# Attention transfers in program order, gate outputs from ScalarE's queue, a dilated merge over more slots, and a first head laid elsewhere

## The chip, the cores and the metric

The kernel runs on one core of one Trainium2 chip. The metric is the device time of one execution in microseconds (us); lower is better. All data are float32; the matmuls take their operands as two parts each (a rounded high part and the rest), so one product is three matmuls: high by high, high by low, low by high.

The engines are named as in the profile: PE is TensorE (PEld its weight loads), DVE is VectorE, ACT is ScalarE, POOL is GpSimd, SP is SyncE, which here only issues transfers. ACT can issue transfers too.

## The reference, cut to what matters

One layer of a bidirectional encoder on a sequence of 1024 positions with a width of 1024:

```python
h = rmsnorm(x, g_mix) * (1 + scale1) + shift1
qa, ka, va, qb, kb, vb, ga, gb = split(h @ w_in)         # 6 x 512 columns, then 2 x 1024 gate columns
oa = mixture_of_dilations(qa, ka, va, rel_bias)          # 8 heads of 64, windows (128,1), (512,4), (2048,16)
ob = neighbourhood_attention_2d(qb, kb, vb, rpb)         # 8 heads of 64, an 8 x 16 window on a 16 x 64 grid
merged = sigmoid(ga) * (oa @ w_branch_dil) + sigmoid(gb) * (ob @ w_branch_na)
x = x + gate1 * (merged @ w_out)
# then rmsnorm, an up projection, a depthwise convolution, a gated product, a down projection, rmsnorm
```

The three dilated patterns of a head are merged for each position by softmax weights over their log sums (`w = softmax(lse)`, `sum(w * o)`).

## The kernel before

The program is traced from Python into one instruction list per engine. A planner places the instructions: it simulates the program and lets an engine's later instruction go ahead of an earlier one where that looks better. Inside `tc.manual_schedule(engines=...)` the engines named keep the order in which the program was written. Waits are put in by the planner. Every transfer counts on one of eight completion counters, given out in turn over both issuing engines, and it waits for the transfer that had the same counter before, so a transfer waits for the landing of the one eight places ahead of it in the planned order.

The stages that matter here, with their times in the profile:

1. *Projections* (to 281 us). Seven pairs of q and k products (`order = (4, 5, 6, 7, 1, 2, 3)`) are computed with a seven-product scheme; `a_operands` prepares the weights of one pair mostly on POOL (sums at lines 441 to 443, subtractions at line 61). Their raw weights come by `p_load` (line 708) alternately into the buffers `wraw` of the pool `w` and `xr` of the pool `lpool`, two buffers each. Results are staged in `qs` tiles and stored from ACT's queue to the scratch tensor `qks` (lines 375 and 393). At the end the first two gate weight tiles (`w_in[24]`, `w_in[25]`) are loaded into `wraw` (line 833).
2. *First loads of the attention* (lines 843 to 853). The pools of the projection are released, and new pools take their place from the same address on: `qk2` (q, k and low k of two heads, each tile 4 KB a partition), then `sm` (the multiplier `lnm`, four `bias` tiles, two `vv` tiles, the probabilities `P`), and, later in the text, `at` (operands `th` and `tl`, outputs `u1` and `u23`, the merge's small tiles `fr`, `fs`, `fa`, `fl`, `fb`). A tile waits for whatever lay at its place before. The first head's loads are written in the order `qk_load(0)`, `lnm`, bias, values, second bias.
3. *Attention* (281 to about 650 us). 102 slots are run in order, each as `settle` (softmax of the scores of the slot before on DVE and ACT, copies of turned tiles), then the lists `first`, `O`, `T`, `S`, `last` of that slot. Eight dilated heads, in four pairs, start eight slots apart (slots 0 to 63 and a tail); eight neighbourhood heads start at slots 64, 68 and so on, four apart. Between the parts of a slot `fill` puts steps of the gate product (`h @ w_in` columns 24 to 39, 256 steps of three matmuls), so that PE has work. After a gate tile of 128 x 512 is done, ACT copies it to a `gs` tile (two buffers, line 1309) and SP stores it to the scratch tensor `gs` (line 1310). ACT, DVE and PE keep program order here; SP and POOL are planned freely.
4. *Merge of a dilated pair*, whose first slot is `s0 = 16 * pr`: `turn` (transpose of the statistics, s0 + 17), `rows` (copy to `fr`, store to the scratch `sts`, line 1121), `spread` (nine reads back in another layout, lines 1125 and 1129, s0 + 19), `factors` (s0 + 20, DVE line 1135 first), `shares` (s0 + 21, ten stores of the weights to `fcs`), `load` (broadcast reads into `fb`), `weigh` (DVE line 1167) and `merge` (POOL line 1176 and the store of the output, line 1177, s0 + 31).
5. *Branch stage* (from about 650 us): outputs are read back (`oraw`), split, and multiplied by `w_br`; gates are read back and passed through a sigmoid.

In the merge the slots are fixed numbers; DVE waits inside `factors` for the reads of `spread`.

Of the kernel before, what the change touches and what calls it, by code (L numbers as in the profile page):

```python
# [10 lines left out]
FT = mybir.dt.float32  # L11
# [8 lines left out]
KT = 8  # L20
# [9 lines left out]
def hybrid_encoder(tc, xT, c, w_ada, small, w_in, p1_bias, p23_bias, na_bias, ln2_mult, ident, w_br, w_out,  # L30
# [57 lines left out]
    halves = [slice(0, 512), slice(512, 1024)]  # L88
# [435 lines left out]
    with tc.manual_schedule(engines={e.engine for e in (sp, act, dve, pool, pe)}):  # L524
# [183 lines left out]
        def p_load(n):  # L708
            pr, r = order[n], []
            for t in (pr, 4 + pr) if pr < 4 else (8 + pr, 12 + pr):  # L710
                r.append(wpool.tile([128, KT, 128], FT, name="wraw") if n % 2 == 0 else
                         lpool.tile([128, KT, 128], FT, name="xr", bufs=2))
                sp.dma_start(r[-1], w_in[t])
            return [t.rearrange("p (a b) m -> p a b m", a=2) for t in r]
# [126 lines left out]
    lpool.release()  # L841
    qkpool.release()
    qk2 = tc.alloc_tile_pool(name="qk2", bufs=2, reuse_waits="tile")
    sm_pool = tc.alloc_tile_pool(name="sm", bufs=2, reuse_waits="tile")
    with tc.manual_schedule(engines={sp.engine, pool.engine}):
        qks = {0: qk_load(0)}
# [28 lines left out]
        act.activation(pp, pp, AF.Exp, bias=mi, scale=-1.0, accum_out=li)  # L875

    gspool = tc.alloc_tile_pool(name="gs", bufs=2, side="right", reuse_waits="tile")
    at_pool = tc.alloc_tile_pool(name="at", bufs=2, reuse_waits="tile")

    turned, scored = [], []  # L880

# [74 lines left out]
    def at(slot, phase, job, *args):  # L956
        slots[slot][phase].append((job, args))

    class DilHead:
        def __init__(self, pair, pr, i, s0, u, st):  # L960
            self.pair = pair
            self.pr, self.i, self.u, self.st, self.head = pr, i, u, st, 2 * pr + i
            self.a = slice(64 * i, 64 * i + 64)
            self.P, self.tt, self.po = {}, {}, {}
            if self.head > 1:
                at(s0 - 5, "first", self.load)
                at(s0 - 8, "first", lambda: qks.update({self.head: qk_load(self.head)}))
            if self.head:
                at(s0 - 3, "first", self.load_v)
                at(s0 - 2, "first", self.prepare)  # L970
                at(s0 - 1, "first", lambda: q_blocks(qks[self.head]))
            at(s0, "first", self.values)
            for n in range(4):
                at(s0 + n, "S", self.far_scores, n)
                at(s0 + n + 2, "T", self.far_turn, n)
                at(s0 + n + 4, "O", self.far_out, n)
                at(s0 + n + 4, "S", self.near_scores, n)
                for js in (((0, 1),), ((2, 3),), ((4, 5),), ((6, 7), (8,)))[n]:
                    at(s0 + n + 6 + (js == (8,)), "T", self.near_turn, js)
                    at(s0 + n + 8 + (js == (8,)), "O", self.near_out, js)  # L980
# [112 lines left out]
    class DilPair:  # L1093
        def __init__(self, pr):
            self.pr, s0 = pr, 16 * pr
            at(s0, "first", self.begin) if pr else self.begin()
            for i in range(2):
                DilHead(self, pr, i, s0 + 8 * i, lambda: self.u, lambda: self.st)
            at(s0 + 17, "T", self.turn)
            at(s0 + 20, "last", self.factors)  # L1100
            at(s0 + 19, "first", self.spread)
            at(s0 + 21, "last", self.shares)
            for z in range(2):
                at(s0 + 22 + z, "first", self.load, 1, z)
            for n, g, z in ((25, 1, 0), (26, 1, 1), (29, 0, 0), (30, 0, 1)):
                at(s0 + n, "last", self.weigh, g, z)
            at(s0 + 31, "first", self.merge)

        def begin(self):
            self.u = [at_pool.tile([128, S], FT, name=n) for n in ("u1", "u23")]  # L1110
# [179 lines left out]
    def fill_steps():  # L1290
# [3 lines left out]
        for n in range(16):  # L1294
# [6 lines left out]
            for hf in range(2):  # L1301
                ensure(marks[-2])
                p = ps_g.tile([128, 512], FT, name="pj")
                for k in range(KT):
                    product(p, w, lambda k: h[hf, k], ks=[k])
                    if k == KT - 1:
                        def out(p=p, n=n, hf=hf):
                            g = gspool.tile([128, 512], FT, name="gs")
                            act.activation(g, p, AF.Copy)
                            sp.dma_start(g_scr[n][:, halves[hf]], g)  # L1310
                        aside(600, out)
                        marks.append(count[0])
                    yield
# [11 lines left out]
    def fill(n, asides=True):  # L1325
        for _ in range(n):
            next(steps, None)
            if asides:
                catch_up(550)
# [4 lines left out]

    att = contextlib.ExitStack()
    att.enter_context(tc.manual_schedule(engines={e.engine for e in (pe, act, dve)}))
    fill(5)
    for s in range(102):
        n = 2 + (s % 4 == 3) if s < 64 else 2 + s % 2 if s < 96 else 1
# [6 lines left out]
        run(slots[s]["last"])  # L1346
        fill(n - (n > 1))
    ensure(count[0])
    at_pool.release()
    sm_pool.release()  # L1350
    ps_a.release()
    ps_l.release()
    qk2.release()
# [62 lines left out]
    mpool = tc.alloc_tile_pool(name="mg", bufs=1, side="right", reuse_waits="tile")  # L1416
    ms = [mpool.tile([128, KT, S], FR, name=n) for n in ("mhi", "mlo")]

    sp_order = contextlib.ExitStack()
    sp_order.enter_context(tc.manual_schedule(engines={e.engine for e in (sp, pool)}))  # L1420
    late = [(j, t) for j in (10, 11) for t in range(KT)]
# [651 lines left out]
```

## Time and profile before

| | |
|---|---|
| median of 3 runs | 1502.94 us (1498.84 to 1503.26) |
| profiled execution, its own time | 1502.36 us |
| its span, first to last instruction | 1500.6 us |
| TensorE busy | 1451.0 us, 97% of the span |
| ScalarE, VectorE, GpSimd busy | 53%, 64%, 56% |
| mean granted TensorE clock | 0.989 |
| transfers | 241.14 MB, mean 161 GB/s |
| share of transfers issued by SP (q1) and ACT (q10) | 220.04 and 19.73 MB |

A row of the timeline has the start in us, the duration in us, the engine, the line of the kernel, the operation, and output <- input with the number of instructions merged; in brackets stands how long the engine had been idle before, and whom it waited for. `SPq` and `ACTq` are the queues that issue transfers; an issue is not the transfer's own time. A row of waits has the waiting group, the group waited for, the sum in us, the number of times and the longest. A row of stretches has the stretch, its length, the busy time of PE, PEld, DVE, ACT and POOL with their instruction counts, the granted TensorE clock (1.00 is full speed), the mean busy share of the 16 DMA engines, and GB/s.

### The profile page before, as it was taken

Reading aid. Unit: us, or ns where it says so; the run is one execution under the profiler, and the core shown is the slowest. Engines: PE = TensorE matmul, PEld = TensorE weight load, DVE = VectorE, ACT = ScalarE, POOL = GpSimd, SP = SyncE. Lnnn points to the kernel's source line nnn. Section 1 sums busy time; section 2 is a strip of 40 time slices with the busy share of each in tenths; the row PEclk is TensorE's granted clock in tenths of the full one; section 3 lists DMA queues with packets and bytes.
Section 4 is the critical chain, followed back from the end, with each engine's and each line's share of the span. In section 5 each row is a group of like instructions: output and inputs, shape, how many; then the busy total and the mean of one; then the engine's idle time right before and its main releaser. Section 6 shows DMA issues by size and latency. Waiting matters only on the chain.

```text
span 1500.6 us, 21335 instructions
## 1 busy us (share of the span) xinstructions
PE 1451.0 (97%) x7308; PEld 1225.1 (82%) x7308; DVE 967.5 (64%) x1809; ACT 790.4 (53%) x1479; POOL 839.4 (56%) x690
## 2 busy tenths in 40 slices
PE   9999999799999699999999999999999999999998
PEld 8877888688888578887888778888888888887788
DVE  7696543256666476657625798666666667787865
ACT  6635543277777466763335555444444447574542
POOL 4165675244451365522257858766666676988712
PEclk9999999899999899999999999999999999999999
DMA  9596345676777989668744413222222234542313
GB/s 368 204 345 210 101 180 197 201 188 164 185 194 190 235 199 265 177 222 271 232 133 154 133 43 107 93 84 77 85 76 85 85 133 143 197 142 69 99 46 113
DMA packets 130516, 241.14 MB, mean 161 GB/s; under 512 B 47812, under 2 KB 60740, under 8 KB 130372
## 3 DMA queue, kind: packets, MB, share of 16 engines
q1 hardware_dynamic: 121752, 220.04, 47.9%
q10 hardware_dynamic: 8656, 19.73, 3.5%
q8 instruction: 58, 0.95, 0.3%
q14 instruction: 50, 0.41, 0.1%
HBM read 185.60 MB, written 59.90 MB: 164 GB/s over the span
## 4 chain that ended last, share of the span: by engine, by line
PE 67%; DMA 9%; DVE 8%; POOL 6%; ACT 5%; issue 3%; SPq 1%; ACTq 0%; DVEq 0%; POOLq 0%
PE pj L497 13%; PE pj L495 13%; PE pj L496 13%; PE pj L84 6%; PE pj L86 6%; PE pj L85 6%; PE T L1021 1%; PE O L1033 1%; POOL wlo L61 1%; DMA oraw<-ob 1%; POOL wsl L61 1%; DMA wraw<-w_down 1%; DMA oraw<-w_ada 1%; PE T L1069 1%; DMA ks<-qks 1%
## 5 line engine op out<-in xcount | busy, mean ns | idle before, releaser
L61 POOL TENSOR_TENSOR wlo<-wraw,whi 128x512 fp32r<-128x512 f32 (+1 forms) x92 | 116.8, 1290 | 132.3 <-ACT whi L57 114.9
L495 PE MATMUL pj<-op,wsh 128*128 128x512 f32 x408 | 158.5, 390 | 1.8 <-ACT wsh L57 1.8
L496 PE MATMUL pj<-op,wsh 128*128 128x512 f32 x408 | 158.9, 390 | 0.5 <-DVE op L1492 0.5
L497 PE MATMUL pj<-op,wsl 128*128 128x512 f32 x408 | 157.4, 389 | 0.0
L61 POOL TENSOR_TENSOR wsl<-big,wsh 128x512 fp32r<-128x512 f32 (+1 forms) x86 | 111.7, 1320 | 45.0 <-ACT wsh L57 40.0
L84 PE MATMUL pj<-h,whi 128*128 128x512 f32 x272 | 117.7, 433 | 0.0
L85 PE MATMUL pj<-h,whi 128*128 128x512 f32 x272 | 108.4, 399 | 0.0
L86 PE MATMUL pj<-h,wlo 128*128 128x512 f32 x272 | 108.2, 398 | 0.0
L1702 DVE SCALAR_TENSOR_TENSOR big<-pj,sm,big 128x512 f32<-128x512 f32 (+2 forms) x183 | 94.9, 563 | 16.5 <-ACT big L1696 15.5
L889 DVE TENSOR_TENSOR tl<-T,th 128x512 fp32r<-128x512 f32 (+3 forms) x120 | 76.1, 649 | 25.9 <-ACT th L885 25.9
L495 PEld LDWEIGHTS pj<-op,wsh 128*128 128x128 f32 x408 | 76.6, 188 | 18.5 <-ACT wsh L57 2.7
L495 PE MATMUL pj<-op,whi 128*128 128x512 f32 x232 | 90.7, 391 | 0.3 <-ACT wc L501 0.3
L496 PE MATMUL pj<-op,whi 128*128 128x512 f32 x232 | 90.5, 390 | 0.2 <-DVE op L1522 0.2
L496 PEld LDWEIGHTS pj<-op,wsh 128*128 128x128 f32 x408 | 76.6, 188 | 17.0 <-DVE op L1492 0.9
L497 PE MATMUL pj<-op,wlo 128*128 128x512 f32 x232 | 90.3, 389 | 0.0
L497 PEld LDWEIGHTS pj<-op,wsl 128*128 128x128 f32 x408 | 76.6, 188 | 15.9 <-POOL wsl L61 0.2
L61 POOL TENSOR_TENSOR wsl<-wraw,wsh 128x384 fp32r<-128x384 f32 (+1 forms) x46 | 56.7, 1254 | 57.7 <-ACT wsh L57 50.0
L874 DVE CUSTOM_DVE_ANT_0 P<-S,bias 128x256 f32<-128x256 f32 x128 | 48.9, 420 | 56.0 <-PE S L1006 36.1
L57 ACT ACTIVATE whi<-wraw 128x1024 fp32r<-128x1024 f32 (+2 forms) x49 | 48.5, 994 | 57.7 <-PE pj L85 28.9
L1250 POOL TENSOR_SCALAR P<-P,stb 128x288 f32<-128x288 f32 (+1 forms) x32 | 41.2, 1286 | 65.4 <-DVE stb L1247 28.1
L875 ACT ACTIVATE P<-P,st 128x256 f32<-128x256 f32 x128 | 64.0, 503 | 25.8 <-DVE st L874 25.6
L1696 ACT ACTIVATE big<-pj,sm 128x512 f32<-128x512 f32 x61 | 47.0, 773 | 54.5 <-DVE pj L516 32.2
(476 smaller groups left out, 4546.6 us busy)
## 6 DMA issues: line engine op xcount, KB each, us to landing
wada<-w_ada SPq DMA_DIRECT2D x31, 512.0 KB
qks<-qs ACTq DMA_DIRECT2D x28, 512.0 KB
wraw<-w_in SPq DMA_DIRECT2D x26, 512.0 KB
big<-w_up SPq DMA_DIRECT2D x22, 512.0 KB
wraw<-w_up SPq DMA_DIRECT2D x22, 512.0 KB
big<-as SPq DMA_DIRECT2D x22, 512.0 KB
as<-big SPq DMA_DIRECT2D x21, 512.0 KB
qs<-qks SPq DMA_DIRECT2D x32, 256.0 KB
```

The costliest lines, as they stand in the source:

```text
L57: act.activation(hi, raw, AF.Copy)
L61: lo_eng.tensor_tensor(lo[:, i:i + step], raw[:, i:i + step], f(hi)[:, i:i + step], OP.subtract)
L84: pe.matmul(psum, whi[:, k0 + k], mhi, start=k == 0, stop=False)
L85: pe.matmul(psum, whi[:, k0 + k], mlo, start=False, stop=False)
L86: pe.matmul(psum, wlo[:, k0 + k], mhi, start=False, stop=k == n - 1)
L495: pe.matmul(psum, whi[:, k], bhi, start=j < 4 and k == 0, stop=False, skip_group_check=True)
L496: pe.matmul(psum, whi[:, k], blo, start=False, stop=False, skip_group_check=True)
L497: pe.matmul(psum, wlo[:, k], bhi, start=False, stop=k == n - 1, skip_group_check=True)
L874: dve.tensor_tensor_reduce(pp, d, bias, -1.0, BIG, OP.add, OP.min, mi)
L875: act.activation(pp, pp, AF.Exp, bias=mi, scale=-1.0, accum_out=li)
L889: dve.tensor_tensor(tt[1][:m, :n], pt[:m, :n], f(tt[0])[:m, :n], OP.subtract)
L1702: dve.scalar_tensor_tensor(y[:, dst], src, wt, y[:, dst], OP.mult, OP.add)
```

## The change

- The raw weights of the seventh pair (`n = 6`) go to `xr` instead of `wraw`.
- The pool `at` is laid out ahead of `sm` (it was behind it), so the tiles of `sm` (bias, values, probabilities) lie higher by the size of `at`, and those of `at` take their place.
- Each dilated head after the second loads its q and k one slot later (s0 - 7).
- The merge: `spread` s0 + 20 (was 19), `factors` s0 + 22 (was 20), `shares` s0 + 23 (was 21), `load` s0 + 25 and 26 (were 22 and 23), `weigh` s0 + 28, 29, 31, 32 (were 25, 26, 29, 30), `merge` s0 + 33 (was 31).
- Gate tiles are stored from ACT's queue, right behind ACT's copy.
- SP keeps program order from the first gate step of the attention until the branch stage's own ordering begins.

```diff
             for t in (pr, 4 + pr) if pr < 4 else (8 + pr, 12 + pr):
-                r.append(wpool.tile([128, KT, 128], FT, name="wraw") if n % 2 == 0 else
+                r.append(wpool.tile([128, KT, 128], FT, name="wraw") if n % 2 == 0 and n < 6 else
                          lpool.tile([128, KT, 128], FT, name="xr", bufs=2))
...
     qk2 = tc.alloc_tile_pool(name="qk2", bufs=2, reuse_waits="tile")
+    at_pool = tc.alloc_tile_pool(name="at", bufs=2, reuse_waits="tile")
     sm_pool = tc.alloc_tile_pool(name="sm", bufs=2, reuse_waits="tile")
...
     gspool = tc.alloc_tile_pool(name="gs", bufs=2, side="right", reuse_waits="tile")
-    at_pool = tc.alloc_tile_pool(name="at", bufs=2, reuse_waits="tile")
...
-                at(s0 - 8, "first", lambda: qks.update({self.head: qk_load(self.head)}))
+                at(s0 - 7, "first", lambda: qks.update({self.head: qk_load(self.head)}))
...
             at(s0 + 17, "T", self.turn)
-            at(s0 + 20, "last", self.factors)
-            at(s0 + 19, "first", self.spread)
-            at(s0 + 21, "last", self.shares)
+            at(s0 + 20, "first", self.spread)
+            at(s0 + 22, "last", self.factors)
+            at(s0 + 23, "last", self.shares)
             for z in range(2):
-                at(s0 + 22 + z, "first", self.load, 1, z)
-            for n, g, z in ((25, 1, 0), (26, 1, 1), (29, 0, 0), (30, 0, 1)):
+                at(s0 + 25 + z, "first", self.load, 1, z)
+            for n, g, z in ((28, 1, 0), (29, 1, 1), (31, 0, 0), (32, 0, 1)):
                 at(s0 + n, "last", self.weigh, g, z)
-            at(s0 + 31, "first", self.merge)
+            at(s0 + 33, "first", self.merge)
...
                             act.activation(g, p, AF.Copy)
-                            sp.dma_start(g_scr[n][:, halves[hf]], g)
+                            act.dma_start(g_scr[n][:, halves[hf]], g)
...
     att.enter_context(tc.manual_schedule(engines={e.engine for e in (pe, act, dve)}))
+    att_sp = contextlib.ExitStack()
+    att_sp.enter_context(tc.manual_schedule(engines={sp.engine}))
     fill(5)
...
     ensure(count[0])
+    sm_pool.release()
     at_pool.release()
-    sm_pool.release()
...
     ms = [mpool.tile([128, KT, S], FR, name=n) for n in ("mhi", "mlo")]
 
+    att_sp.close()
     sp_order = contextlib.ExitStack()
```

## The prediction

> **What bounds the kernel now.** I read the page's first part, then a table of stretches over the attention (281 to 648 us), where all edits lie.
>
> ```profile
> PE 1451.0 (97%) x7308; PEld 1225.1 (82%) x7308; DVE 967.5 (64%) x1809; ACT 790.4 (53%) x1479; POOL 839.4 (56%) x690
> ...
> 281.00:296.00 15.00, 6.27 (x18) 4.73 (x18) 1.47 (x8) 2.18 (x7) 4.44 (x6) 0.66 0.81 246
> 300.00:507.80 207.80, 204.82 (x1299) 182.05 (x1297) 128.40 (x412) 150.54 (x419) 80.14 (x75) 1.00 0.75 193
> 507.80:520.60 12.80, 0.42 (x3) 0.07 (x2) 2.79 (x10) 2.32 (x7) 0.00 (x0) 0.64 0.73 173
> 520.60:525.20 4.60, 4.60 (x15) 3.99 (x16) 4.46 (x8) 2.65 (x8) 3.93 (x4) 0.51 1.07 247
> 525.20:648.00 122.80, 115.20 (x741) 102.45 (x741) 84.59 (x244) 83.45 (x222) 70.02 (x62) 1.00 0.79 199
> ```
>
> The columns are the stretch, its length, busy time of PE, PEld, DVE, ACT and POOL, the granted clock, the DMA share and GB/s. TensorE is the bound nearly everywhere; it does no work to spare in this change, so only time in which it stands or runs slowly can be won. Two such places show: the opening of the attention (281 to 300) and a hole at 508. The waits of TensorE name their causes:
>
> ```profile
> PE T L1259 <- DVE tl L889: 13.9, 4, 12.4
> PE S L1005 <- DMA ks<-qks: 4.4, 1, 4.4
> ...
> PE T L1021 <- ACT P L875: 2.3, 2, 2.2
> PE S L1006 <- DMA kl<-qks: 2.3, 1, 2.3
> ...
> PE S L1230 <- DMA kl<-qks: 0.2, 1, 0.2
> ```
>
> Opening: 4.4 + 2.3 + 2.2 = 8.9 us. Hole: 12.4 us. From 300 to 507.8 only 207.80 - 204.82 = 3.0 us are idle, so the eight dilated heads themselves hold nothing to win.
>
> **The hole at 508: the merge's factors.** The timeline of the engines around it:
>
> ```profile
> 520.56 1.06 PE L1259 MATMUL T<-idt,P 128*96 128x128 f32 x4 [12.38 <-DVE tl L889]
> ...
> 498.42 0.28 DVE L1120 COPY fr<-T 64x128 f32<-64x128 f32 x1
> 504.17 0.42 DVE L1250 TENSOR_SCALAR P<-P,stb 128x384 f32<-128x384 f32 x1
> 517.72 0.18 DVE L1135 TENSOR_TENSOR fl<-fs 64x32 f32<-64x32 f32 x1 [13.12 <-DMA fs<-sts]
> ...
> 504.59 0.47 SPq L1121 DMA_DIRECT2D sts<-fr  x1
> 512.86 0.61 SPq L1125 DMA_DIRECT2D fs<-sts  x1
> 513.52 2.89 SPq L1129 DMA_DIRECT2D fs<-sts  x8
> ```
>
> The last pair's statistics are in SBUF at 498.7, but SP issues their store only at 504.59 (loads planned ahead of it go first); the read back follows its landing (512.86) and the last of nine pieces is issued at 516.4. VectorE keeps its order, so it stands at `factors` from 504.6 to 517.72, and behind it stand `tl`, the transposes and TensorE. The change works on both ends. The store goes in program order: the entries ahead of it are those of slots up to 65, so about 499. `spread` moves from slot 19 to 20 of the pair and `factors` from 20 to 22, two slots of about 122.8 / 32 = 3.8 us later, in which VectorE goes on: the point where it waits moves from 504.6 to about 512.2 even without the hole. With the same 512.86 - 504.59 = 8.3 us from issue to landing, the read starts at 507.3 and is issued by 510.8; the last landing took 517.72 - 516.41 = 1.3, so the factors' input is there at 512.1. That ties with the wait's new place, so what could stay is of the size of a late landing, not of 12 us: I let the wait go. `shares`, the loads and `weigh` move one to three slots as well and keep their distances; `merge` moves two, and its store must be away before the pair after next writes the same `u` buffers some four slots later, and before the branch stage reads it 70 us later for the last pair: nothing.
>
> The prize is 12.4 us and the slow clock behind it, 4.6 us at 0.51, worth 4.6 x 0.49 = 2.3: 14.7 us. What is late next is transfers:
>
> ```profile
> 470.00:507.80 37.80, 37.19 (x232) 32.97 (x231) 23.91 (x72) 24.62 (x71) 10.38 (x9) 1.00 0.99 267
> 525.20:618.00 92.80, 86.26 (x552) 76.61 (x552) 63.77 (x190) 62.51 (x168) 53.31 (x47) 1.00 0.98 241
> ...
> SPq L773 <- PE O L1272: 9.4, 1, 9.4
> ```
>
> On both sides the DMA engines are 0.98 busy. In the hole they moved 173 x 12.8 = 2.2 MB for a TensorE that stood; at 241 GB/s these cost 2.2 / 0.241 = 9.2 us. Lower end: all of it comes back as waits, and the hole gives 14.7 - 9.2 = 5.5. Upper end: none, because SP also waits for engines there (9.4 us for an O product), so loads run ahead of need. I take 3 us lost, nearer to the second, since TensorE's one wait on a DMA after 300 is the 0.2 us of L1230: **-11.5 us** (5.5 to 14.7).
>
> **The opening.**
>
> ```profile
> 295.62 0.33 PE L1021 MATMUL T<-idt,P 128*128 128x128 f32 x1 [2.17 <-ACT P L875]
> ...
> 268.58 0.70 DVE L508 TENSOR_TENSOR pj<-pj,ks 128x512 f32<-128x512 f32 x1 [2.03 <-PE pj L497]
> 273.60 0.39 PE L497 MATMUL pj<-h,qb 128*128 128x512 f32 x1
> ...
> 275.06 0.33 SPq L65 DMA_DIRECT2D wraw<-w_in  x1
> 276.69 1.37 SPq L401 DMA_DIRECT2D ks<-qks  x2
> 278.16 2.29 SPq L401 DMA_DIRECT2D kl<-qks  x2
> ...
> SPq L65 <- POOL wlo L950: 13.1, 1, 13.1
> SPq L848 <- DMA qks<-qs: 3.6, 1, 3.6
> ```
>
> SP stood 13.1 us at L65 for a gate weight tile, the fourth (`w_in[27]`), which is not needed until much later, with the first head's query and key loads behind it. In program order that weight comes after them. Their own tiles lie on `ks` and `qb` slots of the projection, free at 268.58 + 0.70 = 269.3 and at 273.60 + 0.39 = 274.0. So `ks` can go 7.4 us earlier and `kl` 4.2 us earlier, with 0.5 MB less ahead of them. The bias and value loads, behind them, go earlier by the same 4.2 to 7.4 us, since with `at` laid first their tiles fall on operand tiles of the projection instead of staging tiles whose stores land late. Not all gets free: the 3.6 us of L848 is a wait of a load from `ln2_mult` on a store to another tensor, which only shared completion counters explain (the program has eight, given out in turn, and each transfer waits for the one eight places before), and those stay. The transpose at 295.62 then comes at 288.2 to 291.4. TensorE without waits would be there at 295.62 - 8.9 - 2.2 = 284.5, so a wait of 3.7 to 6.9 stays. The slow clock:
>
> ```profile
> 288.60:293.00 4.40, 4.40 (x15) 3.72 (x14) 0.40 (x3) 0.00 (x0) 1.44 (x2) 0.50 0.83 211
> 293.00:296.40 3.40, 1.06 (x6) 0.43 (x6) 1.06 (x8) 2.58 (x7) 3.40 (x5) 1.00 0.80 241
> 296.40:299.80 3.40, 3.40 (x13) 2.91 (x12) 0.83 (x5) 1.97 (x7) 3.40 (x4) 0.50 1.05 239
> ```
>
> 4.4 and 3.4 us at half speed cost 2.2 + 1.7 = 3.9 us. The second came after a stretch with a longest wait of 2.17 us, so short waits cost clock too, and waits of 3.7 to 6.9 remain: I count 1 of the 3.9 as won. Bounds 4.2 and 7.4 + 3.9 = 11.3; I take 5.5 + 1, **-6.5 us**, in the lower half because the DMA share of these stretches is 0.8 and more already.
>
> The Trainium skill ("TensorE: Matmul & The Clock Gate", Part 1) says that the clock is halved after at least one idle window of about 3.4 us. The trace halves it at 296.4 after a window in which TensorE was busy for 1.06 of 3.40 us, so it does not quite agree. By the page's rule scattered short waits would cost no clock, the opening would give 5.5 + 3.9 = 9.4, and the sum below would be 1484.
>
> **Its cover: raw weights of the seventh projection.** They move from `wraw` to `xr`. The second `xr` buffer, which holds the half that POOL adds up first, comes free late:
>
> ```profile
> 239.64 2.54 POOL L61 TENSOR_TENSOR kl<-xr,kl 128x512 fp32r<-128x512 f32 x2 [0.88 <-ACT kl L57]
> 229.97 1.29 POOL L441 TENSOR_TENSOR ks<-wraw 128x512 f32<-128x512 f32 x1 [3.07 <-DMA wraw<-w_in]
> ...
> 225.67 0.33 SPq L713 DMA_DIRECT2D wraw<-w_in  x1
> ...
> 260.56 0.60 ACT L501 ACTIVATE wc<-pj 128x512 f32<-128x512 f32 x1 [1.17 <-PE pj L497]
> ```
>
> That is at 242.2. A load took 229.97 - 225.67 = 4.3 us, so POOL's work for this projection starts at 246.5 instead of 229.97. TensorE's first step of it ends with the copy at 260.56, so it starts 12 matmuls of 1451 / 7308 = 0.2 us earlier, at 258.2, and needs three sums and two subtractions of 1.3 us and one copy of 1.06 before: 246.5 + 7.6 = 254.1, with 4.1 us to spare. The later operands are asked for 2.4 us apart, about what a pair of subtractions takes. So nothing; if the load takes twice as long, 0.2 us.
>
> **Gate outputs from ScalarE's queue.**
>
> ```profile
> L1310 SPq DMA_DIRECT2D gs<-gs x32: 319/390/3924, 297.6 to 673.0; - x32
> SPq L1310 <- ACT gs L1309: 18.3, 7, 11.3
> 561.78 0.58 ACT L1309 ACTIVATE gs<-pj 128x512 f32<-128x512 f32 x1
> 571.64 0.41 SPq L1310 DMA_DIRECT2D gs<-gs  x1
> ```
>
> SP loses 32 x 0.39 = 12.5 us of issue and 18.3 us of waiting; ScalarE gains the issue. It has 207.8 - 150.5 = 57 us and 122.8 - 83.5 = 39 us idle in the two long stretches, which hides it. But a write on ScalarE waits for the transfer eight before it too, and behind it wait the exponentials, `th`, and TensorE. In most rows SP waits for the copy, so that transfer had landed; in the worst, SP came 571.64 - 562.36 = 9.3 us after the copy. From 0 to about 6 us; I take **+2**, for the crowded stretch after 470.
>
> **Sum:** -11.5 - 6.5 + 2 = -16 on the profiled execution's 1502.36: 1486.4. The median of the runs is 0.6 above it, so **1487 us**.
>
> **Rivals.**
> - *Transfers take the hole's place*: the hole gives 5.5, the opening 4.2, ScalarE costs 2: -7.7, 1495. For it: the share of 0.98; against: SP's waits on engines.
> - *All of it goes* and ScalarE hides its part: 14.7 + 11.3 = 26, 1477.
> - *The order is not the cause*: SP's queue merely mirrors the landings (8.3 us for 32 KB of statistics), and the waits come again two slots later: 1503. Against: the 13.1 us at L65 is plainly order.
> - *Slower*: ScalarE's writes are held by transfers eight before. If SP runs late by five us at each of the 13 writes after 470, ScalarE stands 65 us; its 39 idle us cover a part, 26 reach TensorE: -18 + 26 = +8, 1511. It decides from 4.4 us a write on, where 13 x 4.4 = 57 = 39 + 18 eats the whole gain. For it: the row at 571.64; against: the other rows.
>
> **Chances.** Forecast 0.49 (1480 to 1492); transfers 0.22; all 0.12; order 0.09; ScalarE 0.08. The range leaves out the last and the upper half of the fourth, and reaches the second and third: 1475 to 1501. A measurement of this kernel tells 0.3% (4.5 us) from nothing: faster 0.82, same 0.10, slower 0.08.
>
> **What would show it.** Right: no TensorE wait over 3 us on `tl` near slot 68 to 71; the store L1121 issued within 2 us of its copy; the first `ks` load issued ahead of the fourth gate weight, before 272; clock 1.00 through 500 to 530. Wrong: waits of TensorE on `ks`, `bias` or `vv` from 500 to 620 (transfers), ScalarE waiting before L1310 (slower rival), or a wait on operands of the seventh projection near 258.

## The result: slower by 0.9%, and the profile after

The changed kernel takes 1515.08 us (1513.61 to 1515.86) beside 1502.35 us of the kernel before on the same chip: a ratio of 1.0088, interval 1.0070 to 1.0106. The forecast was 1487. The profiled execution of the changed kernel took 1514.76 us (span 1513.0). The first line of its page, and stretches with the columns of the prediction's table:

```profile
PE 1456.3 (96%) x7308; PEld 1230.2 (81%) x7308; DVE 965.3 (64%) x1809; ACT 792.8 (52%) x1479; POOL 841.3 (56%) x690
```

```profile
281.00:296.00 15.00, 9.52 (x47) 7.74 (x46) 3.67 (x18) 6.22 (x18) 10.50 (x12) 0.89 0.92 231
300.00:469.20 169.20, 163.91 (x1040) 145.05 (x1039) 100.92 (x332) 125.44 (x346) 68.94 (x64) 1.00 0.64 166
469.20:498.00 28.80, 24.02 (x150) 20.66 (x148) 15.97 (x44) 16.18 (x45) 5.47 (x5) 1.00 0.91 253
498.00:530.00 32.00, 22.61 (x119) 19.42 (x119) 16.30 (x49) 15.23 (x42) 11.28 (x11) 0.86 0.89 227
530.00:578.20 48.20, 40.95 (x233) 36.15 (x234) 30.92 (x93) 28.77 (x77) 22.62 (x19) 0.88 0.82 202
```

The opening is better (9.52 us of work in its 15 us at a clock of 0.89, where it was 6.27 us at 0.66). The one deep hole has become a long shallow one: from 469 to 578 TensorE works 24.02 + 22.61 + 40.95 = 87.6 of 109 us, part of it at a clock of 0.86 to 0.88. The same 502 matmuls in the kernel before, and here as one row:

```profile
472.00:571.00 99.00, 82.79 (x502) 72.75 (x501) 63.84 (x185) 57.85 (x159) 40.21 (x34) 0.93 0.92 225
...
469.20:578.20 109.00, 87.58 (x502) 76.23 (x501) 63.20 (x185) 60.18 (x163) 39.38 (x34) 0.91 0.86 223
```

So 10.0 us are lost, and only 5.2 of them are more standing time. The other 4.8 are the same matmuls taking longer: the clock is granted at 0.50 for 6.8 us three times (from 500.8, 528.1 and 552.0), each time out of a wait of TensorE of 4.0 to 6.2 us, where the kernel before had one slow stretch, in and behind its hole. The waits over 281 to 690 us say who is late:

```profile
DVE P L1240 <- DMA bias<-na_bias: 21.6, 6, 6.6
...
PE T L1259 <- DVE tl L889: 11.7, 6, 4.7
...
DVE u L1167 <- DMA fb<-fcs: 9.3, 5, 4.3
...
PE T L1115 <- DVE tl L889: 8.0, 3, 6.2
```

The wait on the factors' input (15.2 us) is gone. In its place VectorE waits 21.6 us for neighbourhood bias tiles and 9.3 us for the `fb` tiles, neither of which it did before, and TensorE stands behind VectorE as it did.

**A ledger by matmuls.** In both kernels TensorE runs the same 7308 matmuls in the same order, so the start of the k-th in one trace less its start in the other is what was won or lost up to there. Differences per stretch, in us, worked out from the matmul starts of one trace each; minus is a gain. The column "end" is the time in the kernel before at which the stretch ends (the last row goes on to the end of the span); e1 to e18 are the experiments below (in e16, some 150 matmuls before the attention stand in another order, none after). Executions of one kernel differ by up to 14 us here (e5 and e6: 1499 to 1513), so a difference of a few us in one trace is a hint, and one that returns in many columns is more.

```
matmuls         end  after    e2     e6     e7     e8     e3     e5    e11    e14    e15    e16    e17    e18
   0 to 1300  260.7   +0.2   -1.7   +0.2   +0.3   -1.5   -1.3   -1.0   -1.6   +0.0   -0.9   +1.3   -1.2   +0.5
1300 to 1500  312.5   -6.7   -6.3   +0.7   +0.4   -0.6   -6.5   -6.4   -6.4   -5.1   -4.9   -0.9   -6.0   -6.4
1500 to 2500  472.1   +3.6   +3.3   +2.8   +0.7   +0.1   +0.2   +3.0   +0.3   +6.6   +5.1   +0.1   -0.1   +3.6
2500 to 2700  504.9  +12.1   +7.9   +7.8   +3.6   +0.0  +10.8  +10.4  +11.9   +1.1   -0.2   +0.0   -0.2   -0.1
2700 to 2750  530.2  -15.4  -10.0   -8.0  -15.9   +0.7  -16.0  -12.9  -16.0  -15.5  -15.9  -10.0  -16.0   -7.9
2750 to 3000  571.0  +13.4   +6.4   +5.8  +12.3   -0.1  +13.0   +5.5  +12.5  +14.0   +9.3   -0.1   +7.5   -0.1
3000 to 3500  653.1   +1.8   +2.2   -0.2   -0.2   -1.7   +2.2   +2.7   +5.0   +0.8   -0.8   +1.5   -0.3   -1.3
3500 to 3600  675.8   +4.3  +11.5   +0.6   +1.2   +1.9  +14.2   +4.6   +1.8   +4.1   +1.7   -0.0   +2.0   +1.5
3600 to 7308 1500.6   -0.8   +0.3   -1.2   -0.9   -1.2   -0.3   -2.5   -0.9   -0.9   -1.4   -3.0   -4.5   -3.2
sum                  +12.4  +13.6   +8.4   +1.4   -2.5  +16.3   +3.4   +6.6   +5.2   -8.0  -11.2  -18.8  -13.5
```

Read the column "after". The opening gives 6.7 us. The hole's own place gives 15.4. But 12.1 us are lost just ahead of it, 13.4 just behind it, 3.6 in the dilated heads and 4.3 at the entry to the branch stage. How the first two come about is seen in SP's queue and, behind it, on VectorE and TensorE (timeline, as in the prediction):

```profile
483.81 1.33 SPq L1162 DMA_DIRECT2D fb<-fcs  x2
485.19 3.04 SPq L422 DMA_DIRECT2D v<-vbc  x4
488.42 1.25 SPq L1162 DMA_DIRECT2D fb<-fcs  x2
...
491.17 0.83 SPq L1218 DMA_DIRECT2D bias<-na_bias  x2
...
502.07 0.33 SPq L1218 DMA_DIRECT2D bias<-na_bias  x1
...
485.85 0.69 DVE L1167 TENSOR_TENSOR u<-u,fb 128x512 f32<-128x512 f32 x1 [4.33 <-DMA fb<-fcs]
...
500.88 0.46 DVE L1240 CUSTOM_DVE_ANT_0 P<-S,bias 128x288 f32<-128x288 f32 x1 [4.11 <-DMA bias<-na_bias]
...
502.47 0.39 PE L1115 MATMUL T<-idt,st 128*64 128x128 f32 x1 [6.16 <-DVE tl L889]
...
552.42 0.56 DVE L1240 CUSTOM_DVE_ANT_0 P<-S,bias 128x384 f32<-128x384 f32 x1 [6.61 <-DMA bias<-na_bias]
...
554.22 1.08 PE L1259 MATMUL T<-idt,P 128*128 128x128 f32 x4 [4.04 <-DVE tl L889]
```

The first bias tile of the neighbourhood heads is asked for at 491.17, as it is written, one slot (some 3.8 us) ahead of its scores and behind reads of the merge. VectorE stands for it until 500.88, 9.7 us after the request, and TensorE until 502.47. At 552 the same happens again. In the kernel before the planner had put the first two of these loads 69 and 48 us earlier:

```profile
422.56 0.44 SPq L1218 DMA_DIRECT2D bias<-na_bias  x1
...
442.82 0.54 SPq L1218 DMA_DIRECT2D bias<-na_bias  x1
...
490.55 0.34 SPq L1218 DMA_DIRECT2D bias<-na_bias  x1
```

There they were used from 494.0 on without a wait on a transfer. The experiments test three theories: loads late because SP keeps program order; gate writes that hold ScalarE; the spread merge running into the neighbourhood heads. Each time is the median, each ratio is to the kernel before on the same chip, with its 95% interval.

### The profile page after: what moved, and what is told of

It reads as the page before. It is cut to its first block, busy times and chain, and to the rows that moved or that the text cites. A ratio compares the mean times of both kernels' runs of the same rounds, so it can differ in the third digit from the quotient of the medians.

```text
span 1513.0 us, 21241 instructions
## 1 busy us (share of the span) xinstructions
PE 1456.3 (96%) x7308; PEld 1230.2 (81%) x7308; DVE 965.3 (64%) x1809; ACT 792.8 (52%) x1479; POOL 841.3 (56%) x690
## 4 chain that ended last, share of the span: by engine, by line
PE 46%; DVE 3%; DMA 2%; POOL 2%; ACT 1%; issue 1%; SPq 0%; DVEq 0%; POOLq 0%; ACTq 0%
PE pj L495 10%; PE pj L496 10%; PE pj L497 10%; PE pj L86 5%; PE pj L84 5%; PE pj L85 5%; DMA wraw<-w_down 1%; DVE big L460 1%; POOL wsl L61 0%; DVE big L1705 0%; DMA oraw<-ob 0%; ACT wsh L57 0%; DVE op L1606 0%; POOL big L441 0%; ACT whi L57 0%
## 5 line engine op out<-in xcount | busy, mean ns | idle before, releaser
L885 ACT ACTIVATE th<-T 128x512 fp32r<-128x512 f32 (+3 forms) x120 | 65.2, 561 | 20.4 <-ACT gs L1309 5.7
```

What stands on the lines that cost most here:

```text
L885: act.activation(tt[0][:m, :n], pt[:m, :n], AF.Copy)
```

## One part of the change at a time

**e2, order alone.** The kernel before, with

```diff
+    att_sp = contextlib.ExitStack()
+    att_sp.enter_context(tc.manual_schedule(engines={sp.engine}))
...
+    att_sp.close()          # where the changed kernel has it, in the branch stage
```

> The kernel before with one part of the change alone: SP's queue of the attention in program order. Gate writes stay on SP, merge slots and layout as before. Theory (late loads): slower than before, 1508 to 1530, with waits of VectorE on bias tiles of 10 us or more after 480, which the kernel before does not have, and the hole at 508 shorter or gone. Rivals 1 and 2 (gate writes on ScalarE; spread merge): neither is in this kernel, so it is 1490 to 1503, with the hole at 508 closed by the order alone.

Measured: 1522.41 us, 1.0140 (1.0108 to 1.0171). VectorE waits 21.6 us on bias tiles, as the theory of late loads had it. The ledger adds what it had not: the opening gives 6.3, but the largest loss, 11.5, lies after the attention (matmuls 3500 to 3600), and a gate store in program order makes SP wait for its copy:

```profile
SPq L1310 <- ACT gs L1309: 70.0, 13, 16.6
```

In the kernel before this row was 18.3 us. The opening's 6.3 us without the new layout are as much as the changed kernel has with it.

**e6, gate writes alone.** The kernel before, with `act.dma_start(g_scr...)` in place of `sp.dma_start(g_scr...)`.

> The kernel before with one part of the change alone: the 32 gate writes leave from ScalarE's queue. SP stays with the planner, merge slots and layout as before. With SP planned again the changed kernel still took 1514 us, and its ScalarE stood at th and vv behind loads (fb 9.1 us, bias 4.9 us) that neither reads: what stands between them is a gate write. Theory now (two costs: late loads where SP keeps program order, gate writes that hold ScalarE where SP runs ahead): slower than before, 1506 to 1515, with 10 us or more of such waits of ScalarE on loads. Rival 2 (spread merge is the cost of both): no change beyond 3 us, 1498 to 1503. Rival 3 (the layout): the same, 1498 to 1503.

Measured: 1508.42 us, 1.0056 (1.0034 to 1.0077). Slower, as expected, and here is the stall itself, on ScalarE:

```profile
490.55 0.60 ACT L1309 ACTIVATE gs<-pj 128x512 f32<-128x512 f32 x1 [1.29 <-PE pj L86]
495.27 0.33 ACTq L1310 DMA_DIRECT2D gs<-gs  x1
495.64 0.60 ACT L885 ACTIVATE th<-T 128x512 fp32r<-128x512 f32 x1 [4.49 <-DMA v<-vbc]
```

The copy is done at 491.15, the write goes at 495.27, and the `th` behind it has idled 4.49 us until a transfer landed that neither reads: the one eight places ahead. In the trace both transfers count on the same completion counter. The 4.5 us are about the price at which the prediction's slower rival decides (4.4 us a write). But few writes meet it; over 281 to 690 us the waits of this kind are

```profile
ACT th L885 <- DMA v<-vbc: 4.5, 1, 4.5
...
ACT th L885 <- DMA wraw<-w_in: 3.9, 2, 2.9
...
ACT th L885 <- DMA vv<-v: 3.4, 1, 3.4
```

and some of about 1 us. The Trainium skill ("DMA: Bandwidth & Descriptors", section "Issuing engines are not separate DMA queues") says that transfers run on the same 16 engines whoever issues them and that a second issuer saves only the time to issue. Of that the trace shows the time to issue, 0.39 us a write on SP; beside it SP is rid of its waits for the copies (18.3 us in the kernel before), and ScalarE has the waits above.

**e7, slots alone.** The kernel before with the merge's new slots (spread 20, factors 22, shares 23, load 25 and 26, weigh 28, 29, 31, 32, merge 33).

> The kernel before with one part of the change alone: the dilated merge on its new slots. SP stays with the planner, gate writes on SP, layout as before. Theory (two costs, SP's order and ScalarE's gate writes; the spread is the good part): the wait on the factors' input at 508 (13.1 us) falls below 5 us and the time to 1488 to 1497. Rival 2 (the spread merge runs into the neighbourhood heads): slower than before, 1505 to 1515, with waits of VectorE or TensorE from 500 to 600 that sum to more than 12 us.

Measured: 1502.67 us, 1.0010 (0.9993 to 1.0027). Both expectations miss. The hole's place gives 15.9 us, and 12.3 + 3.6 come back around it, mostly where `weigh` now waits for `fb`, which it did not before:

```profile
DVE u L1167 <- DMA fb<-fcs: 10.6, 8, 2.8
```

Nor is the wait on the factors gone (5.41 us): the planner's SP issues the store 7.6 us after its copy (5.9 before), and the read back follows 8.8 us later (8.3). This suggests that the wait on the factors was the place where the stretch's lack showed and not its cause; e16 below bears it out.

**e8, layout alone.** The kernel before with `at` ahead of `sm`, the seventh projection's weights on `xr`, q and k at s0 - 7.

> The kernel before with the smallest parts alone: the first head's tiles laid elsewhere, the seventh projection's weights on the xr buffers, the query and key loads seven slots ahead and not eight. Theory (two costs elsewhere): the opening gains little while the planner still puts the fourth gate weight ahead of the head's loads, 1496 to 1504, with the hole at 508 as it was. Rival 3 (the layout is a cost): 1506 to 1515, with new waits in the opening or on key loads.

Measured: 1503.12 us, 1.0020 (1.0006 to 1.0034): under the 0.3% that the prediction takes as the least it can tell from nothing. The layout gives the opening nothing by itself; the order does.

## One part of the change taken back

**e1, SP planned again.** The changed kernel without the lines of `att_sp`.

> The changed kernel, but SP's queue of the attention is ordered by the planner again, as in the kernel before; gate writes on ScalarE, the merge's new slots and the new layout stay. Theory (late loads: in program order the neighbourhood bias tiles are asked for one slot before their scores, behind stores and reads of the merge that make SP wait; in the kernel before the planner had asked for them up to 77 places earlier): VectorE's waits on bias tiles (21.6 us in the changed kernel) fall below 5 us, and the time falls from 1515 to 1485 to 1500. Rival 1 (ScalarE's gate writes hold the exponentials): they are still there, so 1508 to 1516. Rival 2 (the merge spread over more slots runs into the neighbourhood heads): still there too, 1508 to 1516.

Measured: 1514.18 us, 1.0087 (1.0059 to 1.0115). The theory of late loads alone falls: VectorE's waits on bias tiles are gone, and the kernel is as slow as with them. It still has the gate writes on ScalarE, which alone cost 8.4 us (e6).

**e3, gate writes on SP again.** The changed kernel with `sp.dma_start(g_scr...)`.

> The changed kernel with the 32 writes of the gate outputs back on SP, in program order there. Rival 1 (ScalarE's gate writes hold the exponentials): faster than the changed kernel by 8 to 20 us, 1495 to 1507. Theory (late loads): SP has 32 more issues of 0.39 us and waits for their copies, so its loads come later still: 1515 to 1530, with more waiting of VectorE on bias tiles than the 21.6 us now. Rival 2 (spread merge): no change beyond a few us, 1511 to 1520.

Measured: 1519.64 us, 1.0127 (1.0110 to 1.0145). Rival 1 falls, and VectorE's waits on bias tiles grow to 28.9 us, as the theory had it. In program order a gate store costs on either queue: on ScalarE 3.6 us in the dilated heads (0.2 here), on SP the branch stage, 14.2 us (4.3 there):

```profile
632.90 17.38 SPq L1310 DMA_DIRECT2D gs<-gs  x2
653.45 0.32 SPq L1287 DMA_DIRECT2D ob<-u  x1
653.82 0.42 SPq L65 DMA_DIRECT2D wraw<-w_br  x1
654.30 2.27 SPq L1371 DMA_DIRECT2D oraw<-oa  x4
```

**e11, order up to slot 92.** e3 with

```diff
     for s in range(102):
+        if s == 92:
+            att_sp.close()
```

> The changed kernel with gate writes on SP (1519.6 us), and program order on SP up to slot 92 only, so that the loads for the branch stage can pass the last gate writes. In the kernel it is compared with, 14 us are lost after the last neighbourhood scores, between its matmuls 3500 and 3600, where SP stands 17 us at a gate write with the branch loads behind it. Theory (program order carried past the attention): 9 us or more of the 14 come back, 1506 to 1511. Rival (the branch stage's loads are late for lack of transfers or of their buffers): 1515 to 1520.

Measured: 1510.27 us, 1.0056 (1.0038 to 1.0073). The 14.2 us shrink to 1.8: the loss at the branch stage was `oraw` behind stores that wait for ScalarE and VectorE.

**e4, old merge slots.** The changed kernel with the merge as before.

> The changed kernel with the dilated merge on its old slots. SP in program order, gate writes on ScalarE, new layout. Theory (two costs, SP's order and ScalarE's gate writes): the merge's factors are late again (VectorE waits 8 to 15 us on them) and the late bias loads stay: 1513 to 1525. Rival 2 (the spread merge runs into the neighbourhood heads): 1495 to 1508.

Measured: 1509.26 us, 1.0065 (1.0042 to 1.0089). Below the theory's range and above its rival's. By the medians the new slots cost 5.8 us in the changed kernel, though the intervals of the two overlap (1.0070 to 1.0106 there); e18 shows a kernel where they gain.

**e5, bias three slots ahead.** The changed kernel with

```diff
-                at(s0 + n - 1, "first", self.bias, cb)
+                at(s0 + n - 3, "first", self.bias, cb)
```

> The changed kernel with one number changed: the bias tiles of the neighbourhood heads are asked for three slots ahead of their scores and not one. SP stays in program order. Theory (late loads): VectorE's waits on bias tiles (21.6 us) fall below 5 us; those on the merge's factors tiles (9.3 us) stay. TensorE's loss of 480 to 560 (some 20 us) goes for the most part: 1495 to 1505. If something else of the order is as late as the bias (values, keys, factors), it takes its place and 1507 to 1513 comes out. Rivals 1 and 2: bias waits shift to other waits, 1511 to 1516.

Measured: 1507.42 us, 1.0045 (1.0026 to 1.0065). The waits on bias tiles go from 21.6 to 1.5 us, and what is lost behind the hole from 13.4 to 5.5. What is lost ahead of it stays (10.4). So the short lead is 7.7 us by the medians (6.5 by the ratios), less than the theory's 10 us or more, and something else sits at matmuls 2500 to 2700.

## What crowds the stretch ahead of the neighbourhood heads

In slots 54 to 61 `vb_chunks` copies the neighbourhood values from `vbc` to `v` inside DRAM: 16 copies of 192 or 256 KB, 3.6 MB, each with an issue of about 0.58 us. They come there because their destination overlays the dilated heads' values. Three kernels move them:

```diff
+    vb_scr = dram.tile([64 * sum(NA_NC), 512], FT, name="vbs")
-    vb_s = [v_scr[64 * ...
+    vb_s = [vb_scr[64 * ...
-    for n, cb in zip((54, 56, 59, 61), (0, 3, 1, 2)):
+    for n, cb in zip((20, 26, 32, 38), (0, 3, 1, 2)):
```

**e9**: e7 with it. 

> The kernel before with the merge on its new slots (alone that made no difference), and the 16 copies that rearrange the neighbourhood values in DRAM (3.6 MB) put into a tensor of their own and issued from slots 20 to 38 of the dilated heads, where the DMA engines are 0.71 busy, not from 54 to 61, just ahead of the stretch in which they are 0.96 to 1.0 busy. Theory now (the stretch from the seventh dilated head to the third neighbourhood head is short of transfers, so a wait closed there comes back as others): 3.6 MB / 0.24 = 15 us of transfers fewer there; most of the 12 us hole is won, 1487 to 1494. Rival (order alone is the cause: each load late behind something that waits, however many bytes): 1498 to 1504.

Measured: 1493.84 us, 0.9954 (0.9936 to 0.9971), within the theory's range.

**e16**: the kernel before with it. 

> The kernel before with the values rearranged early alone, merge on its old slots. Theory (the hole at 508 has a queue of loads ahead of the statistics' store; with 3.6 MB fewer near it, it shortens but stays, as the store's place is the planner's): 1493 to 1500; the spread merge then adds a few us to the gain (1493.8 with both). Rival (bytes alone are the cause, the slots do nothing): 1490 to 1495, as with both. If the spread is what counts: 1499 to 1503.

Measured: 1491.19 us, 0.9952 (0.9936 to 0.9968). Faster than the theory with nothing else changed, in the range of its rival (bytes alone), and the new slots of e9 add nothing to it: the 12.4 us wait is down to 2.83 and no loss stands beside it.

```profile
511.00 0.89 PE L1260 MATMUL T<-idt,P 128*96 128x128 f32 x4 [2.83 <-DVE tl L890]
...
499.20 0.47 SPq L1122 DMA_DIRECT2D sts<-fr  x1
503.36 0.62 SPq L1126 DMA_DIRECT2D fs<-sts  x1
```

These two rows say how. The statistics' store goes 5.4 us earlier than in the kernel before (499.20, was 504.59), 0.03 us after its copy, and the read back follows it by 4.2 us and not by 8.3. Both its wait in SP's queue and the time from its issue to the read back have become shorter.

**e14**: the changed kernel with it. 

> The changed kernel, with the neighbourhood values rearranged in a tensor of their own at slots 20 to 38. Theory (the 12 us lost ahead of the neighbourhood heads are in part the 16 copies of 3.6 MB, which in program order also hold SP for 16 issues of 0.58 us, 9 us): 6 to 12 us of it come back, 1503 to 1509. Rival (late bias loads and gate writes on ScalarE are the whole of it): 1511 to 1516.

Measured: 1508.42 us, 1.0063 (1.0042 to 1.0084). The 12.1 us ahead of the hole become 1.1, with VectorE's waits for `fb` down from 9.3 to 2.5 us; the 14.0 behind it stay, with the late bias tiles:

```profile
DVE P L1241 <- DMA bias<-na_bias: 19.6, 5, 6.0
```

The row "2500 to 2700" is the cleanest of the ledger: in every kernel with these copies moved it is between -0.2 and +1.1; with them in place, each of the parts (order 7.9, gate writes 7.8, slots 3.6) makes a loss there. How much of it is their bytes and how much their 9 us of SP's issue time was not separated; no kernel had the one without the other, and the copies also got a tensor of their own in each.

## Where program order pays

**e10**: e3 with program order given up at slot 40. 

> The changed kernel with gate writes on SP (that took 1519.6 us) and SP's program order given up from slot 40 on: the opening and the first dilated heads in program order, everything from the crowded stretch on with the planner. Theory (program order pays in the opening, 6.5 to 8 us, and costs from the neighbourhood heads on): the opening keeps its 6 to 8 us, the rest is as in the kernel before with the merge on its new slots, which was even: 1492 to 1497. Rival (the gain of the opening is always given back where transfers are short, since TensorE only arrives there earlier): 1499 to 1505.

Measured: 1502.33 us, 1.0001 (0.9988 to 1.0014). The theory misses by 5 us: 6.4 us are lost in the dilated heads (by the ledger's working), 5.6 of them near 445 us. The planner's SP then runs ahead with a neighbourhood bias tile and keys, waits 5.93 us at a gate store, and the second pair's `fb` comes behind them:

```profile
422.38 1.54 SPq L1218 DMA_DIRECT2D bias<-na_bias  x1
424.01 1.14 SPq L401 DMA_DIRECT2D qs<-qks  x2
...
426.49 5.93 SPq L1310 DMA_DIRECT2D gs<-gs  x1
...
433.67 2.56 SPq L1162 DMA_DIRECT2D fb<-fcs  x4
```

**e12**: e10 with the values at slots 20 to 38. 

> The kernel with SP in program order up to slot 40, gate writes on SP, the merge on its new slots and the new layout, and the neighbourhood values rearranged at slots 20 to 38 in a tensor of their own. If both theories hold (order pays in the opening, bytes are short in the crowded stretch), the gains add: 6 to 8 and 6 to 13, 1480 to 1489. If only the order counts, 1492 to 1498; if only the bytes, 1487 to 1494; if neither, 1499 to 1505.

Measured: 1498.12 us, 0.9979 (0.9963 to 0.9996). The two gains do not add: the loss in the dilated heads is 11.7 us here, by the same working.

**e13**: e12 with the hand-over at slot 4. 

> As the kernel with SP in program order up to slot 40 and the values early (1498.1 us), but program order ends at slot 4, where no merge is under way. There 7.4 us were ahead after the opening and 11.7 us were lost near slot 40, where the planner put bias and key loads ahead of the factors tiles of the second pair. Theory (the loss is that of the hand-over in the middle of a merge): it goes, and opening and values add: 1482 to 1490. Rival (what the opening wins is given back wherever the planner's SP runs ahead): 1493 to 1500.

Measured: 1496.44 us, 0.9975 (0.9961 to 0.9989). By the ledger's working no loss in the dilated heads (0.2), but no gain in the opening either (0.9, where e12 has 6.2): its waits on `ks` and `kl` are back (3.8 and 2.2 us). In e10 and e13 the rival's times came, but its reason does not hold in general: e17, below, keeps the opening's gain to the end.

**e15**: order kept up to slot 92, and every cost found so far taken out: gate writes on SP, bias three slots ahead, values at slots 20 to 38. 

> The changed kernel with all that the runs so far blame taken out and the order kept: SP in program order up to slot 92, gate writes on SP, bias tiles asked for three slots ahead, values rearranged at slots 20 to 38. Theory (program order itself is harmless; what costs are short leads, the writes on ScalarE, the crowding and the branch loads behind the last gate writes): the opening's 7.7 us last, 1488 to 1497. Rival (a queue that waits at every store of the merge loses whatever the leads): 1500 to 1508.

Measured: 1491.65 us, 0.9945 (0.9923 to 0.9967). Program order as such is not the loss, as the theory had it.

**e17**: e15 with the values at slots 5, 8, 11, 14. 

> As the kernel with order and leads (1491.7 us), with the values rearranged at slots 5 to 14, before the first merge begins, and not at 20 to 38. Theory (the 5 us lost at 430 to 440 are these copies beside the second pair's merge): they are won, 1484 to 1489. Rival (program order loses at some merge whatever lies beside it): 1490 to 1496.

Measured: 1484.92 us (1483.89 to 1487.54), 0.9906 (0.9887 to 0.9925), the fastest of all, ahead of the kernel before and of the changed one. The 5.1 us of e15 in the dilated heads are gone. The first line of its page, and TensorE's largest waits:

```profile
PE 1447.4 (98%) x7308; PEld 1224.2 (83%) x7308; DVE 958.8 (65%) x1809; ACT 790.1 (53%) x1479; POOL 841.6 (57%) x690
```

```profile
PE T L1022 <- ACT P L877: 5.7, 1, 5.7
PE T L1260 <- DVE tl L890: 5.1, 5, 3.2
```

**e18**: e17 with the old merge slots. 

> As the kernel before it in this list, with the merge on its old slots (factors 20, spread 19, merge 31). Theory (in program order the statistics' way out and back takes longer than the three slots that the old places leave, so the spread is worth something with this order, though nothing with the planner's): VectorE waits 5 us or more on the factors' input, 2 to 8 us slower than with the new slots, 1487 to 1495. Rival (the slots do nothing once the bytes are out of the way): within 2 us of it.

Measured: 1493.07 us, 0.9961 (0.9947 to 0.9975). Here the new slots are worth 8 us by the medians:

```profile
DVE fl L1136 <- DMA fs<-sts: 14.7, 4, 5.2
```

With the planner they were worth nothing (e7), in the changed kernel they are worse by the medians alone (e4). In program order the way out and back of the statistics needs the two slots more, once nothing else is late.

Not run was the planner's SP with the copies at slots 5 to 14. So what program order is worth in e17 beyond the opening (6.0 us there, 0.9 in e16) is not shown.

## Why the prediction was wrong, point by point

- **The opening: right.** Forecast -6.5, measured -6.7, and by the mechanism told, SP's order: `kl` goes at 274.33 (forecast 274.0) and the transpose comes at 289.44 (288.2 to 291.4), 6.2 us earlier where 5.5 were counted. One wait of 5.46 us stays (3.7 to 6.9 were forecast). One slow stretch is left of two, and the clock gives the other 0.5 us of the 6.7, where 1 was counted. Two details were not as told: `ks` goes at 262.93, 6 us before the time at which the prediction read its tile as free (269.3), and the new layout is not needed (e2 has 6.3 us without it).

```profile
262.93 2.62 SPq L401 DMA_DIRECT2D ks<-qks  x2
274.33 1.67 SPq L401 DMA_DIRECT2D kl<-qks  x2
...
289.44 1.39 PE L1021 MATMUL T<-idt,P 128*128 128x128 f32 x4 [5.46 <-ACT P L876]
```

```profile
289.40:293.00 3.60, 3.55 (x13) 2.92 (x14) 0.11 (x1) 2.53 (x8) 3.60 (x4) 0.56 0.99 230
...
296.40:300.00 3.60, 3.60 (x27) 3.33 (x26) 0.93 (x5) 0.81 (x3) 0.06 (x1) 1.00 0.96 192
```

- **The hole, -11.5: the step that failed.** Its mechanism came as told: the store L1121 went 0.03 us after its copy, and the wait at `factors` is gone. What failed is "so loads run ahead of need. I take 3 us lost". I read SP's waits on engines as proof that loads were early. They were, because the planner had moved them, and the same edit took that lead away. The prediction priced SP's order only for the loads that it brings forward (the statistics, the first head), and for none that it puts back. Measured over matmuls 2500 to 3000: +10.1 in place of -11.5 (14.7 less 3 is 11.7; the sum carries 11.5). With the leads given back and the copies out of the way the same matmuls give -8.7 (e17), so the size of the prize was not far off.
- **The lower bound, 5.5, was no bound.** It let the hole's own 2.2 MB come back, and nothing beyond. The lack was that of a stretch into which 3.6 MB of copies fall; it could cost more than the hole (12.1 + 13.4 against 15.4), and moving the copies in the kernel before gains 0.48% (0.32 to 0.64%), some 7 us, with no other edit (e16).
- **ScalarE, +2 (0 to 6): mis-sized.** Alone it costs 8.4 us (e6). The slower rival, given 8%, had the right mechanism and nearly the right price for one write, but in e6 three writes meet it at 2.9 to 4.5 us, and others at about 1, not 13 at 5. In the changed kernel it is 3.4 us in the dilated heads and more than paid back where SP would stall instead (e3).
- **No step at all for the branch stage**, where the order goes on past the attention: 4.3 us, 14.2 with gate stores on SP.
- **The dilated heads "hold nothing to win"**: true, and 3.6 us to lose, to ScalarE's writes (e3: 0.2).
- **The seventh projection: covered**, as forecast; up to matmul 1300 the difference is 0.2 us.
- **The tests named.** The store went within 2 us of its copy and `ks` before 272, as the signs of being right say. But TensorE waited over 3 us on `tl`, and the clock was to be 1.00 through 500 to 530 and was 0.86 from 498 to 530: the sum had counted 2.3 us of slow clock as won, and more of it came (4.8 us over the 502 matmuls above). The waits named as the sign of failure came, on bias tiles, though VectorE stood at them and TensorE behind it on `tl`.

## What to carry to other kernels

When an edit pins a queue's order, list every load that the free order had issued well ahead of its place in the program and give each its own lead back, in the program; the trace of before shows them as loads with long gaps before their use. A long wait in a stretch whose transfers are always busy is where the lack shows, not what it is: look first for traffic in that stretch that could run at another time. Measure the edits alone and together: here the same slots were worth nothing in one kernel, less than nothing by the medians alone in another, and 8 us in a third, depending on what else was late.

## What was not expected of the hardware

A busy share of the DMA engines above 0.9 stood for very different rates. In the crowded stretch of the kernel before (472 to 571, share 0.92) and at the entry to the branch stage of the changed one (660 to 680, share 0.97), the packets were:

```profile
DMA packets 16871, 22.30 MB, mean 225 GB/s; under 512 B 9847, under 2 KB 9911, under 8 KB 16861
```

```profile
DMA packets 3279, 6.83 MB, mean 341 GB/s; under 512 B 331, under 2 KB 331, under 8 KB 3279
```

With 58% of the packets below 512 B the engines move 225 GB/s, with 10% they move 341. The Trainium skill ("DMA: Bandwidth & Descriptors", section "Specifications") asks for 512 B or more for full rate, and these two stretches fit it. They differ in what is moved as well, so packet size is not shown to be the only reason. Either way the 241 GB/s by which the prediction turned bytes into time is the rate of what moved in that stretch, not a limit of the engines. That one queue's transfer holds another's was told before the result; that a single ScalarE write stands 4.1 us for it (491.15 to 495.27) was not measured then.

The slow clock followed TensorE's busy share, not the length of a single wait. In all the traces the clock changes in steps of 3.41 us. Cut 250 to 700 us into such windows, aligned with the changes, and take TensorE's busy share of each from its matmul rows. At full clock, each of the 81 windows with a share below 0.44 was followed by one at 0.50, of the 66 windows from 0.44 to 0.65 only 11 were, and of the 2354 above 0.65 none. A slow window was followed by a full one in all 89 cases of 0.86 busy or more, in 2 of 7 between 0.75 and 0.86, and in none of 41 below. So the waits of 4 to 6 us in the changed kernel cost clock three times where the one hole of 12 us cost it once.
